# Six quarter-tile places for split weights, and a new order of the seven products of a pair, in a hybrid decoder trunk

## The chip, the cores and the metric

The kernel runs on one core of a Trainium2 chip. The metric is the device time of one execution in microseconds (us): the median over several runs. A time "of the profiled execution" is that of the single run in which the hardware profiler also recorded every instruction; its span runs from the first to the last instruction.

## The reference

The kernel computes two decoder layers on 512 tokens of width 1024. Layer 0 mixes by a gated DeltaNet, layer 1 by sliding-window attention, and each layer also attends to 256 memory tokens. The change touches only the feed-forward block that ends each layer (D_MODEL 1024, D_FF 2816):

```python
def swiglu(h, w_gate_up, w_down):
    gu = h @ w_gate_up
    return (jax.nn.silu(gu[..., :D_FF]) * gu[..., D_FF:]) @ w_down
...
        x = x + swiglu(rms_norm(x, ln_ffn[layer]), w_gate_up[layer], w_down[layer])
```

## The kernel before

Activations lie transposed: channels on the 128 partitions, 512 tokens along the row. Every matrix product is made from a high and a low part of both operands: `split` makes the high part by an ACT copy into the fp32r type (`whi`, line 137) and the low part by a VectorE (DVE) subtraction of it (`wlo`, line 150). `mm3` then issues three matmuls for each block of 128x128 weights: high times high, high times low activation, low weight times high activation. So a product can start when `whi` is there, and its third matmul needs `wlo`.

The 22 column blocks of gate and of up are done in two halves of 11 (`f0`). Each half first makes one block plainly (`project`, 24 matmuls of 512 tokens), then goes by pairs of blocks through `quarters`: a gate pair (its result is scaled by `rstd` and put through silu, tile `fg`) and then an up pair (its result is multiplied by the gate's, tile `fu`, and split into activations `acts` by `put`). The first pair of gates in each layer is made plainly, too, so there are 18 gate pairs and 20 up pairs: 38 pairs of `quarters`. After each half the down projection follows (`pj` tiles, matmuls of 512 tokens).

`quarters` does a pair of blocks over two halves of the 512 tokens with seven instead of eight block products. Each product is 4 x 3 = 12 matmuls of 256 tokens; they are named here by the key of the activation that they use: 11, 21, t1, t2, 22, t3, t4. The raw weights of a pair are `a1` (128x1024, tag `wraw`, its halves for 11 and 21), `s1` and `s3` (two sums, tag `ws`, which a POOL DMA makes by adding a second block while it loads) and `last` (for t4). Two DVE additions turn `a1` in place into the weights of t2 and 22. The split weights lie in tiles `whi` and `wlo` of 128x1024, three buffers of each, and a pair takes four: `w0` (11 and 21), `two` (t1 and t3), `w2` (t2 and 22) and `w3` (t4).

Results pass through three PSUM banks of the tag `g` for each pair (six in all): `pa` for 11, t2, t3 and t4 in turn, `pb` for 21, `pc` for t1 and 22. Where a later product is added onto a bank whose value so far is also wanted (11 and t1 and t2), `held` first copies it out (ACT, tile `fs`). So t2 waits for the copy of 11, t3 for the copy of t2, 22 for the copy of t1, and t4 for the DVE operation that reads the bank after t3.

The order of the work on each engine is fixed when the program is built: a scheduler places the instructions of all engines by its own estimate of when they are ready, within the dependencies. Each engine then runs its list strictly in order, and waits for others by semaphores. Loads are issued by the SP queue, the adding loads by POOL.

Of the kernel before, what the change touches and what calls it, by code (L numbers as in the profile page):

```python
# [9 lines left out]
F32 = mybir.dt.float32  # L10
F32R = mybir.dt.float32r
I32 = mybir.dt.int32
AF = mybir.ActivationFunctionType
# [5 lines left out]
P = 128  # L19
T = 512  # L20
# [65 lines left out]
class Builder:  # L86
# [742 lines left out]
    def ffn(self, fp, xp, layer, h, apool, rope=False):  # L829
# [1 line left out]
        nc, a = self.nc, self.a  # L831
        acc = self.acc
        half = FT // 2
        acts, sums = [], []

        col = lambda f, up: a["wgu"][layer, 2 * f + up]

        def gate(f):
            ps = self.project(col(f, 0), h, "pj")
            if f == 0:  # L840
                self.rstd_from(acc)
                self.use(SILU_SIN)
            g = self.t(fp, [P, T], F32, "fg", 4)
            self.tt(nc.vector, g, ps, self.rstd, ALU.mult)
            self.fn(g, g, AF.Silu)
            return g

        def gates(f):
            g = self.quarters(fp, [col(f + i, 0) for i in range(2)], sums, (self.rstd, self.rstd), "fg", 4)
            for x in g:  # L850
                self.fn(x, x, AF.Silu)
            return g

        def put(u):
            n = len(acts)
            acts.append(self.pair(apool) if n < KD else self.pair(fp, f"ac{n}"))
            self.split(u, *acts[-1])

        def add(x, ps, t=slice(0, T)):
            d = self.t(fp, [P, T], F32, "fu", 3)[:, t]  # L860
# [2 lines left out]

        for f0 in (0, half):
            acts.clear()
            g = gate(f0)
            u = self.t(fp, [P, T], F32, "fu", 3)
            self.tt(nc.vector, u, self.project(col(f0, 1), h, "g"), g, ALU.mult)
            put(u)
            for f in range(f0 + 1, f0 + half, 2):  # L870
                if f == 1:
                    g = []
                    for i in range(2):
                        for _ in range(2 - i):
                            sums.append(self.token_sums(fp, layer, len(sums), h))
                        g.append(gate(f + i))
                    sums.append(self.token_sums(fp, layer, len(sums), h))
                else:
                    g = gates(f)
                for u in self.quarters(fp, [col(f + i, 1) for i in range(2)], sums, g, "fu", 3):  # L880
                    put(u)
            self.acc = None
            tail = KD - 2 if f0 and layer else KD
            down = lambda m, j, n, **kw: self.weight(a["wdn"][layer, m][:, (f0 + j) * P:(f0 + j + n) * P], **kw)
            for m in range(tail):
                ps = self.bank("pj")
                for j, n in ((0, 6), (6, 5)):
                    w = down(m, j, n)
                    for k in range(n):
                        self.mm3(ps, w, k, acts[j + k], j + k == 0, j + k == half - 1)  # L890
                add(self.x[m], ps)
                if f0:
                    self.acc = self.accumulate(xp, self.acc, self.x[m], m)
                if rope and f0 == 0 and m == 0:
                    self.rope_tables(fp)
# [49 lines left out]
        parts["21"], parts["22"] = ([x[:, i * q:(i + 1) * q] for x in h[j + 4]] for i in range(2))  # L945
        return parts

    def quarters(self, fp, src, sums, by, tag, bufs):

        nc = self.nc  # L950
        q = T // 2
# [6 lines left out]
        nc.gpsimd.dma_start(s3, a21, accum_op=ALU.add)  # L958
        last = self.t(fp, [P, T], F32, "wraw", 2)
        nc.sync.dma_start(last, a22)  # L960
        w0 = self.weight(None, raw=a1)
        two = [self.t(self.wpool, [P, D], F32R, t, 3) for t in ("whi", "wlo")]
        w1, w4 = ([x[:, i * T:(i + 1) * T] for x in two] for i in range(2))
        self.split(s1, *w1)

        self.tt(nc.vector, a1[:, :T], s1, a1[:, :T], ALU.add)
        self.tt(nc.vector, a1[:, T:], a1[:, :T], a1[:, T:], ALU.add)
        w2 = self.weight(None, raw=a1)
        self.split(s3, *w4)
        w3 = self.weight(None, raw=last)  # L970
        pa, pb, pc = (self.bank("g")[:, :q] for _ in range(3))

        def product(ps, w, i, b, first):

            for j in range(4):
                self.mm3(ps, w, 4 * i + j, sums[j][b], first and j == 0, j == 3, not first)

        def held(ps):
            o = self.t(fp, [P, q], F32, "fs", 3)
            self.copy(o, ps)  # L980
            return o

        u = [self.t(fp, [P, T], F32, tag, bufs) for _ in range(2)]
        product(pa, w0, 0, "11", True)
        p1 = held(pa)
        product(pb, w0, 1, "21", True)
        self.tt(nc.vector, u[0][:, :q], pb, p1, ALU.add)
        product(pc, w1, 0, "t1", True)
        p5 = held(pc)
        product(pa, w2, 0, "t2", False)  # L990
        u2 = held(pa)
        product(pc, w2, 1, "22", False)
        self.tt(nc.vector, u[0][:, q:], pc, u2, ALU.add)
        self.tt(nc.vector, u[0], u[0], by[0], ALU.mult)
        product(pa, w4, 0, "t3", False)
        self.stt(u[1][:, q:], pa, -1.0, p5, ALU.mult, ALU.subtract)
        self.tt(nc.vector, u[1][:, q:], u[1][:, q:], by[1][:, q:], ALU.mult)
        product(pa, w3, 0, "t4", False)
        self.stt(u[1][:, :q], pa, -1.0, by[1][:, :q], ALU.mult, ALU.mult)
        return u  # L1000

    def rstd_from(self, acc, t=slice(0, T)):
        self.use(LN_EXP)
# [208 lines left out]
```

## Time and profile before

| | |
|---|---|
| median of 3 runs | 1216.53 us (1214.99 to 1218.32) |
| profiled execution | 1217.5 us, span 1215.7 us |
| TensorE matmuls (PE), weight loads (PEld) | 1164.1 us (96%), 1003.6 us (83%) |
| VectorE (DVE), ACT, POOL | 818.1 us (67%), 616.0 us (51%), 83.2 us (7%) |
| mean granted TensorE clock | 0.996 |
| DMA | 151.22 MB, mean 124 GB/s |

Columns of the trace's views: a row of the timeline gives start, duration, engine, source line, operation, tiles (output <- inputs), and in brackets the idle time of the engine before it with what ended it. "PE" is the matmul, "PEld" the load of its stationary operand, which goes ahead of it; matmuls are pipelined, so their durations overlap and the distance between starts is what one costs. The chain of waits is followed back from the last instruction, at each step to what released it. The time for the feed-forward pairs lies in four stretches, which begin at about 339, 511, 859 and 1031 us of the span.

### The profile page before, as it was taken

How to read it: one execution, taken by the hardware profiler on the slowest of the kernel's cores; microseconds unless marked ns; L12 is line 12 of the kernel's file. 1: busy time of each engine (PE TensorE's matmuls, PEld its weight loads, DVE VectorE, ACT ScalarE, POOL GpSimd, SP SyncE). 2: the span in 40 equal slices, each digit the busy share in tenths (PEclk: the TensorE clock that was granted, in tenths of full speed). 3: DMA queues.
4: the chain of work that ended last, by engine and by line, in shares of the span. 5: the costliest groups of instructions: out<-in, count | busy, mean ns of one | idle time of the engine just before them, and what ended most of it. 6: DMA issues, size and time to landing. Idle time of an engine off the chain costs nothing.

```text
span 1215.7 us, 19269 instructions
## 1 busy us (share of the span) xinstructions
PE 1164.1 (96%) x7410; PEld 1003.6 (83%) x7410; DVE 818.1 (67%) x1482; ACT 616.0 (51%) x1174; POOL 83.2 (7%) x93
## 2 busy tenths in 40 slices
PE   7999999999999999999999999999999999999997
PEld 6888777877898988888988876788898888898886
DVE  6753977667877775477765767768678644677644
ACT  7578562565555532255543546766455422555423
POOL 0310000000111101011100000010111100111000
PEclk9999999999999999999999999999999999999999
DMA  7424252324556536456533420153466633666232
GB/s 294 140 88 138 88 126 75 121 78 154 167 139 165 142 102 164 115 142 168 135 84 96 130 87 28 44 139 104 119 152 169 156 96 99 151 154 163 75 98 89
DMA packets 72944, 151.22 MB, mean 124 GB/s; under 512 B 16732, under 2 KB 19444, under 8 KB 72852
## 3 DMA queue, kind: packets, MB, share of 16 engines
q1 hardware_dynamic: 61908, 130.06, 35.1%
q0 software_dynamic: 10944, 19.93, 10.2%
q8 instruction: 58, 0.95, 0.3%
q14 instruction: 34, 0.28, 0.1%
HBM read 143.00 MB, written 6.96 MB: 123 GB/s over the span
## 4 chain that ended last, share of the span: by engine, by line
PE 82%; DVE 10%; ACT 3%; issue 3%; DMA 1%; SPq 0%; DVEq 0%; ACTq 0%
PE pj L143 42%; PE g L143 32%; PE sc L143 6%; DVE wlo L150 5%; PE pt L147 1%; ACT fs L137 1%; PE g L147 1%; DVE fu L150 1%; DVE fg L150 1%; ACT sm L131 1%; DMA wraw<-in_wmk 1%; DVE btmp L150 1%; ACT whi L137 0%; DVE big L150 0%; DMA big<-basein 0%
## 5 line engine op out<-in xcount | busy, mean ns | idle before, releaser
L137 ACT ACTIVATE whi<-wraw 128x1024 fp32r<-128x1024 f32 (+3 forms) x249 | 225.6, 921 | 254.2 <-PE pj L143 173.4
L150 DVE TENSOR_TENSOR wlo<-wraw,whi 128x1024 fp32r<-128x1024 f32 (+3 forms) x249 | 259.6, 1054 | 96.3 <-ACT whi L137 95.4
L143 PE MATMUL pj<-h,whi 128*128 128x512 f32 (+1 forms) x676 | 266.1, 395 | 0.2
L143 PE MATMUL pj<-h,wlo 128*128 128x512 f32 (+1 forms) x676 | 265.1, 392 | 1.1 <-DVE wlo L150 1.1
L143 PE MATMUL pj<-l,whi 128*128 128x512 f32 (+1 forms) x676 | 265.5, 393 | 0.0
L143 PE MATMUL g<-T,whi 128*128 128x256 f32 x1216 | 222.8, 281 | 0.0
L143 PEld LDWEIGHTS g<-T,whi 128*128 128x128 f32 x1216 | 187.3, 189 | 0.4
L143 PE MATMUL g<-T,wlo 128*128 128x256 f32 x608 | 171.7, 282 | 0.7 <-DVE wlo L150 0.7
L143 PE MATMUL g<-h,wlo 128*128 128x256 f32 (+1 forms) x516 | 150.2, 302 | 18.9 <-DVE wlo L150 18.9
L143 PE MATMUL g<-h,whi 128*128 128x256 f32 (+1 forms) x516 | 154.5, 302 | 7.6 <-ACT fs L137 7.6
L143 PEld LDWEIGHTS pj<-h,wlo 128*128 128x128 f32 x676 | 127.4, 188 | 29.4 <-DVE wlo L150 2.9
L143 PE MATMUL g<-l,whi 128*128 128x256 f32 (+1 forms) x516 | 150.4, 294 | 0.0
L143 PEld LDWEIGHTS pj<-h,whi 128*128 128x128 f32 x676 | 127.1, 188 | 28.1 <-issue 2.6
L143 PEld LDWEIGHTS pj<-l,whi 128*128 128x128 f32 x676 | 127.2, 188 | 26.6 <-issue 1.5
L137 ACT ACTIVATE fs<-g 128x256 f32<-128x256 f32 x114 | 43.8, 384 | 152.1 <-PE g L143 151.9
L143 PEld LDWEIGHTS g<-h,wlo 128*128 128x128 f32 x516 | 95.3, 189 | 28.2 <-DVE wlo L150 25.8
L143 PEld LDWEIGHTS g<-T,wlo 128*128 128x128 f32 x608 | 114.5, 188 | 1.1 <-DVE wlo L150 1.1
L143 PEld LDWEIGHTS g<-h,whi 128*128 128x128 f32 x516 | 97.6, 189 | 17.1 <-ACT fs L137 14.2
L143 PEld LDWEIGHTS g<-l,whi 128*128 128x128 f32 x516 | 97.8, 190 | 2.9 <-issue 0.5
L957 POOL DMA_DIRECT2D ws<-in_wgu x38 | 33.2, 873 | 951.8 <-DVE wlo L150 259.5
L150 DVE TENSOR_TENSOR fu<-g,fs 128x256 f32<-128x256 f32 x40 | 17.0, 425 | 64.2 <-PE g L143 64.2
L150 DVE TENSOR_TENSOR fu<-pj,rstd 128x512 f32<-128x512 f32 (+1 forms) x34 | 22.4, 659 | 49.9 <-PE pj L143 49.9
(346 smaller groups left out, 1671.3 us busy)
## 6 DMA issues: line engine op xcount, KB each, us to landing
wraw<-in_wgu SPq DMA_DIRECT2D x50, 512.0 KB, 4.1
ws<-in_wgu SPq DMA_DIRECT2D x76, 256.0 KB, 2.9
ws<-in_wgu POOLq DMA_DIRECT2D x76, 256.0 KB, 6.3
wraw<-in_win SPq DMA_DIRECT2D x26, 512.0 KB, 3.6
wraw<-in_wdn SPq DMA_DIRECT2D x32, 384.0 KB, 3.2
wraw<-in_wdn SPq DMA_DIRECT2D x32, 320.0 KB, 2.9
wraw<-in_wgu SPq DMA_DIRECT2D x38, 256.0 KB, 6.0
wraw<-in_wout SPq DMA_DIRECT2D x16, 512.0 KB, 3.6
```

Source lines behind the costliest of these rows:

```text
L131: ins = self.nc.scalar.activation(out, in_, func, **kw).ins
L137: self.copied = self.nc.scalar.activation(out, in_, AF.Copy, **kw).ins
L143: return self.nc.tensor.matmul(out, lhsT, rhs, start=start, stop=stop, skip_group_check=more).ins
L147: return self.nc.tensor.transpose(out, in_, self.ident[:k, :k]).ins
L150: return eng.tensor_tensor(out=out, in0=a, in1=b, op=op).ins
L957: nc.gpsimd.dma_start(s1, a22, accum_op=ALU.add)
```

## The change

Only `ffn` and `quarters` change. The diff, with lines left out where they are context:

```diff
--- before.py
+++ after.py
@@ -831,7 +831,7 @@
         nc, a = self.nc, self.a
         acc = self.acc
         half = FT // 2
-        acts, sums = [], []
+        acts, sums, open_pairs, places = [], [], [], []
 
         col = lambda f, up: a["wgu"][layer, 2 * f + up]
 
@@ -845,17 +845,37 @@
             self.fn(g, g, AF.Silu)
             return g
 
-        def gates(f):
-            g = self.quarters(fp, [col(f + i, 0) for i in range(2)], sums, (self.rstd, self.rstd), "fg", 4)
-            for x in g:
-                self.fn(x, x, AF.Silu)
-            return g
-
         def put(u):
             n = len(acts)
             acts.append(self.pair(apool) if n < KD else self.pair(fp, f"ac{n}"))
             self.split(u, *acts[-1])
 
+        def ring():
+
+            if not places:
+                for _ in range(3):
+                    two = [self.t(self.wpool, [P, D], F32R, t, 3) for t in ("whi", "wlo")]
+                    places.extend(tuple(x[:, i * T:(i + 1) * T] for x in two) for i in range(2))
+            places.append(places.pop(0))
+            return places[-1]
+
+        def begin(f, up, by, tag, bufs, then):
+
+            o = [self.t(fp, [P, T], F32, tag, bufs) for _ in range(2)]
+            steps = self.quarters(fp, [col(f + i, up) for i in range(2)], sums, by, o, ring)
+            next(steps)
+            end()
+            next(steps)
+            open_pairs.append((steps, then, o))
+            return o
+
+        def end():
+            if open_pairs:
+                steps, then, o = open_pairs.pop()
+                next(steps, None)
+                for x in o:
+                    then(x)
+
         def add(x, ps, t=slice(0, T)):
             d = self.t(fp, [P, T], F32, "fu", 3)[:, t]
             self.tt(nc.vector, d, ps, self.rstd[:, t], ALU.mult)
@@ -863,6 +883,7 @@
 
         for f0 in (0, half):
             acts.clear()
+            places.clear()
             g = gate(f0)
             u = self.t(fp, [P, T], F32, "fu", 3)
             self.tt(nc.vector, u, self.project(col(f0, 1), h, "g"), g, ALU.mult)
@@ -876,9 +897,9 @@
                         g.append(gate(f + i))
                     sums.append(self.token_sums(fp, layer, len(sums), h))
                 else:
-                    g = gates(f)
-                for u in self.quarters(fp, [col(f + i, 1) for i in range(2)], sums, g, "fu", 3):
-                    put(u)
+                    g = begin(f, 0, (self.rstd, self.rstd), "fg", 4, lambda x: self.fn(x, x, AF.Silu))
+                begin(f, 1, g, "fu", 3, put)
+            end()
             self.acc = None
             tail = KD - 2 if f0 and layer else KD
             down = lambda m, j, n, **kw: self.weight(a["wdn"][layer, m][:, (f0 + j) * P:(f0 + j + n) * P], **kw)
@@ -945,7 +966,7 @@
         parts["21"], parts["22"] = ([x[:, i * q:(i + 1) * q] for x in h[j + 4]] for i in range(2))
         return parts
 
-    def quarters(self, fp, src, sums, by, tag, bufs):
+    def quarters(self, fp, src, sums, by, u, ring):
 
         nc = self.nc
         q = T // 2
@@ -958,46 +979,41 @@
         nc.gpsimd.dma_start(s3, a21, accum_op=ALU.add)
         last = self.t(fp, [P, T], F32, "wraw", 2)
         nc.sync.dma_start(last, a22)
-        w0 = self.weight(None, raw=a1)
-        two = [self.t(self.wpool, [P, D], F32R, t, 3) for t in ("whi", "wlo")]
-        w1, w4 = ([x[:, i * T:(i + 1) * T] for x in two] for i in range(2))
-        self.split(s1, *w1)
-
-        self.tt(nc.vector, a1[:, :T], s1, a1[:, :T], ALU.add)
-        self.tt(nc.vector, a1[:, T:], a1[:, :T], a1[:, T:], ALU.add)
-        w2 = self.weight(None, raw=a1)
-        self.split(s3, *w4)
-        w3 = self.weight(None, raw=last)
         pa, pb, pc = (self.bank("g")[:, :q] for _ in range(3))
 
-        def product(ps, w, i, b, first):
-
+        def product(ps, raw, b, first):
+
+            w = ring()
+            self.split(raw, *w)
             for j in range(4):
-                self.mm3(ps, w, 4 * i + j, sums[j][b], first and j == 0, j == 3, not first)
+                self.mm3(ps, w, j, sums[j][b], first and j == 0, j == 3, not first)
 
         def held(ps):
             o = self.t(fp, [P, q], F32, "fs", 3)
             self.copy(o, ps)
             return o
 
-        u = [self.t(fp, [P, T], F32, tag, bufs) for _ in range(2)]
-        product(pa, w0, 0, "11", True)
+        product(pa, a1[:, :T], "11", True)
         p1 = held(pa)
-        product(pb, w0, 1, "21", True)
+        product(pc, s1, "t1", True)
+        p5 = held(pc)
+        yield
+
+        self.tt(nc.vector, a1[:, :T], s1, a1[:, :T], ALU.add)
+        product(pa, a1[:, :T], "t2", False)
+        u2 = held(pa)
+        product(pb, a1[:, T:], "21", True)
         self.tt(nc.vector, u[0][:, :q], pb, p1, ALU.add)
-        product(pc, w1, 0, "t1", True)
-        p5 = held(pc)
-        product(pa, w2, 0, "t2", False)
-        u2 = held(pa)
-        product(pc, w2, 1, "22", False)
+        self.tt(nc.vector, a1[:, T:], a1[:, :T], a1[:, T:], ALU.add)
+        product(pc, a1[:, T:], "22", False)
         self.tt(nc.vector, u[0][:, q:], pc, u2, ALU.add)
         self.tt(nc.vector, u[0], u[0], by[0], ALU.mult)
-        product(pa, w4, 0, "t3", False)
+        product(pa, s3, "t3", False)
         self.stt(u[1][:, q:], pa, -1.0, p5, ALU.mult, ALU.subtract)
         self.tt(nc.vector, u[1][:, q:], u[1][:, q:], by[1][:, q:], ALU.mult)
-        product(pa, w3, 0, "t4", False)
+        yield
+        product(pa, last, "t4", False)
         self.stt(u[1][:, :q], pa, -1.0, by[1][:, :q], ALU.mult, ALU.mult)
-        return u
 
     def rstd_from(self, acc, t=slice(0, T)):
         self.use(LN_EXP)
```

Three things are different. First, the split weights of a half's pairs lie in three `whi` and three `wlo` tiles taken once, as six places of a quarter each (128x512), used in turn: each product splits its own 128x512 of raw weights into the next place just before its matmuls in program order. The splits of 1024 columns become two of 512. A place is written again for the sixth product after it. Second, the products come in the order 11, t1, t2, 21, 22, t3, t4. Third, `quarters` is a generator that stops after t1 and after t3: `begin` issues 11 and t1 of a pair, then `end` finishes the pair before it (its t4 and its last operations), and then t2 to t3 of the new pair follow.

How this moves instructions is seen at two places in the first half of layer 0. The first is the hand-over from one pair to the next on PE. The numbers are those of the buffers, in order of creation: g_4000 is bank `pa` of the pair that ends, g_4133 and g_4134 are `pa` and `pb` of the next. Before:

```order
L143 MATMUL g_4000<-T_3283,wlo_3985 128x256
L143 MATMUL g_4133<-h_2803,whi_4113 128x256
L143 MATMUL g_4133<-l_2804,whi_4113 128x256
L143 MATMUL g_4134<-h_2961,whi_4113 128x256
L143 MATMUL g_4134<-l_2962,whi_4113 128x256
L143 MATMUL g_4133<-h_2803,wlo_4114 128x256
L143 MATMUL g_4133<-h_2841,whi_4113 128x256
L143 MATMUL g_4133<-l_2842,whi_4113 128x256
L143 MATMUL g_4133<-h_2841,wlo_4114 128x256
L143 MATMUL g_4000<-T_3182,whi_3996 128x256
```

The first row ends t3 of the old pair. Four matmuls with `whi` of the new pair (two of 11, two of 21) follow, then the first with `wlo`, and after eight matmuls t4 of the old pair. Now, at the hand-over between the pair with bank g_3681 and the one with g_3816 (`pa`) and g_3818 (`pc`); the rows left out are the rest of each product's twelve:

```order
L143 MATMUL g_3681<-T_3283,wlo_3305 128x256
L143 MATMUL g_3816<-h_2803,whi_3304 128x256
L143 MATMUL g_3816<-l_2804,whi_3304 128x256
L143 MATMUL g_3816<-h_2803,wlo_3305 128x256
...
L143 MATMUL g_3816<-h_2921,wlo_3305 128x256
L143 MATMUL g_3818<-T_3182,whi_3306 128x256
...
L143 MATMUL g_3818<-T_3283,wlo_3307 128x256
L143 MATMUL g_3681<-T_3182,whi_3306 128x256
...
L143 MATMUL g_3681<-T_3283,wlo_3307 128x256
L143 MATMUL g_3816<-T_3182,whi_3302 128x256
```

After t3 of the old pair come the twelve of 11 and the twelve of t1 of the new pair, then t4 of the old pair, then t2 of the new one. 21, 22 and t3 follow, and then the next pair's 11: seven products for each pair, everywhere in the same order.

The second place is VectorE's list around the end of an up pair, the results of which are `fu`; `wlo` rows are splits, `wraw` rows the additions in place, `l` rows the splits of activations. Before:

```order
L150 TENSOR_TENSOR fu_4136<-g_4135,fs_4191 128x256
L150 TENSOR_TENSOR fu_4136<-fu_4136,fg_4003 128x512
L150 TENSOR_TENSOR wlo_4253<-wraw_4242,whi_4252 128x1024
L153 SCALAR_TENSOR_TENSOR fu_4137<-g_4133,fs_4177 128x256
L150 TENSOR_TENSOR l_4235<-fu_4136,h_4234 128x512
L150 TENSOR_TENSOR fu_4137<-fu_4137,fg_4004 128x256
L150 TENSOR_TENSOR wlo_4257<-ws_4244,whi_4256 128x512
```

The split of the next pair's first 1024 columns (wlo_4253) stands behind the addition and the multiplication that follow product 22 of the old pair. Now:

```order
L150 TENSOR_TENSOR wlo_3307<-wraw_4070,whi_3306 128x512
L150 TENSOR_TENSOR wraw_4070<-ws_4072,wraw_4070 128x512
L153 SCALAR_TENSOR_TENSOR fu_3805<-g_3816,fg_3670 128x256
L150 TENSOR_TENSOR wlo_3303<-ws_4072,whi_3302 128x512
L150 TENSOR_TENSOR l_4000<-fu_3805,h_3999 128x512
L150 TENSOR_TENSOR wlo_3303<-wraw_3943,whi_3302 128x512
L150 TENSOR_TENSOR fg_3933<-g_3946,fs_3962 128x256
L150 TENSOR_TENSOR wlo_3305<-wraw_4070,whi_3304 128x512
L150 TENSOR_TENSOR fg_3933<-g_3947,fs_4018 128x256
```

Here the pair in work has the results fg_3933, and wraw_4070 belongs to the pair after it: its splits for 11 (first row), t1 (fourth) and t2 (eighth) stand ahead of, or between, the two additions that follow 21 and 22 of the pair in work.

## The prediction

> **What bounds the kernel now.** I read the page's busy shares first, then the chain of waits, then the waits of the weight loads, and last the timeline at the places that these name.
>
> ```profile
> PE 1164.1 (96%) x7410; PEld 1003.6 (83%) x7410; DVE 818.1 (67%) x1482; ACT 616.0 (51%) x1174; POOL 83.2 (7%) x93
> PEclk9999999999999999999999999999999999999999
> ```
>
> PE looks full, but these durations overlap, so the gaps have to be read from starts. The chain of waits in layer 1's first half, for one pair (start, us, what):
>
> ```profile
> 888.98 0.44 DVE fu L150
> ...
> 889.47 0.57 issue
> 890.04 1.23 DVE wlo L150
> 891.27 0.04 issue
> 891.32 5.52 PE g L143 x44
> ...
> 896.86 0.39 ACT fs L137
> 897.25 0.04 issue
> 897.30 2.89 PE g L143 x22
> ...
> 901.35 1.23 DVE wlo L150
> ```
>
> The chain leaves PE twice in a period of 901.35 - 890.04 = 11.31 us. The first time it goes through VectorE: product 22 ends, VectorE adds (888.98), multiplies (the 0.57 called issue) and only then splits the next pair's 1024 columns for 1.23 us. The second time it goes through ACT's copy `fs` of t2, for which t3 waits. The waits of the weight loads over the whole run (us in total, times, longest):
>
> ```profile
> PEld g L143 <- DVE wlo L150: 26.9, 36, 0.8
> PEld g L143 <- ACT fs L137: 14.2, 32, 0.4
> ```
>
> So the loss repeats 36 and 32 times, about once in each of the 38 pairs. What one costs is seen at the starts of the weight loads:
>
> ```profile
> 890.25 0.19 PEld L143 LDWEIGHTS g<-h,whi 128*128 128x128 f32 x1
> 890.37 0.19 PEld L143 LDWEIGHTS g<-l,whi 128*128 128x128 f32 x1
> 891.32 0.19 PEld L143 LDWEIGHTS g<-h,wlo 128*128 128x128 f32 x1 [0.76 <-DVE wlo L150]
> 891.42 0.19 PEld L143 LDWEIGHTS g<-h,whi 128*128 128x128 f32 x1
> ...
> 896.54 0.31 PEld L143 LDWEIGHTS g<-T,whi 128*128 128x128 f32 x2
> 897.29 0.19 PEld L143 LDWEIGHTS g<-h,whi 128*128 128x128 f32 x1 [0.44 <-ACT fs L137]
> 897.40 0.19 PEld L143 LDWEIGHTS g<-T,wlo 128*128 128x128 f32 x1
> ```
>
> Undisturbed, loads start 0.12 us apart (890.25, 890.37). Across the first stall it is 0.95 us, then 0.10: the loss is 0.83 - 0.02 = 0.81 us. Across the second, the last of the two loads of the row at 896.54 starts at 896.66, the next at 897.29, then 897.40: 0.63 - 0.12 - 0.01 = 0.50 us. A pair without either takes 11.31 - 1.31 = 10.0 us, which is 84 matmuls of 0.119 us; a product of twelve takes 1.43 us. The chain's pieces agree: (5.52 - 2.89) / 22 = 0.1195 us for one.
>
> **The change part by part.** *The order of products.* With 1.43 us for each, a bank's earlier value is now read out while other products run: between 11 and t2 lie t1 and the old pair's t4 (2.9 us), between t1 and 22 three products (4.3 us), between t2 and t3 lie 21 and 22 (2.9 us), and between t3 and t4 the next pair's 11 and t1 (2.9 us). What has to fit in is a copy or a VectorE operation of 256 columns:
>
> ```profile
> L137 ACT ACTIVATE whi<-ws x76: 610/614/636, 333.1 to 1131.5; 128x512 fp32r<-128x512 f32 x76
> L137 ACT ACTIVATE fs<-g x114: 383/384/386, 340.2 to 1139.1; 128x256 f32<-128x256 f32 x114
> ```
>
> 0.38 us for the copy, and up to 0.61 us for a split that stands before it on ACT, make 1.0 of 2.9 us. The second stall goes: 32 x 0.50 = 16.0 us. What covers it is two products of other banks; without that cover it costs the 0.50 again.
>
> *The places.* A place is free when the product six before has ended, so 5 x 1.43 = 7.2 us are left for its two halves, 0.61 us on ACT and about 0.69 us on VectorE. That is ample if VectorE's list, which runs strictly in order, gets there. VectorE's own pace, from the starts of neighbours:
>
> ```profile
> 426.23 1.22 DVE L150 TENSOR_TENSOR wlo<-wraw,whi 128x1024 fp32r<-128x1024 f32 x1
> 427.37 0.42 DVE L153 SCALAR_TENSOR_TENSOR fg<-g,fs 128x256 f32<-128x256 f32 x1
> 427.70 0.69 DVE L150 TENSOR_TENSOR wlo<-ws,whi 128x512 fp32r<-128x512 f32 x1
> 428.30 0.42 DVE L150 TENSOR_TENSOR fg<-fg,rstd 128x256 f32<-128x256 f32 x1
> 428.63 0.69 DVE L150 TENSOR_TENSOR wraw<-ws,wraw 128x512 f32<-128x512 f32 x1
> ```
>
> 1.14 us for 1024 columns, 0.60 for 512, 0.33 for 256. Each pair trades two splits of 1024 for four of 512: 4 x 0.60 - 2 x 1.14 = +0.12 us. An up pair then has 12 operations of 512 (seven splits, two additions, one multiplication, two activation splits) and 5 of 256: 7.2 + 1.7 = 8.9 us of the 10.0; a gate pair 10 and 5: 7.7 us. I walked the new list through an up pair, with 0 at the start of its 11, results ready at the ends of products (1.43, 2.9, 4.3, 5.7, 7.2, 8.6, 10.0) and the paces above. As an estimate from these rows the splits are done so: t3's at 2.5 (needed 8.6), 22's at 3.1 (7.2), the next 11's at 3.7 (10.0), the next t1's at 5.4 (11.4), t4's at 7.0 (12.9), the next t2's at 8.4 (14.3). VectorE's reading of t3, behind which t4 stands, is done by 10.7 (12.9). The least slack is 2.2 us. The first stall goes, too: 36 x 0.81 = 29.2 us (two of the 36 are a little shorter; I let that stand against rounding).
>
> *The hand-over to the down projection.* Today its third matmul waits for a split:
>
> ```profile
> 437.88 0.40 PE L143 MATMUL pj<-l,whi 128*128 128x512 f32 x1
> 438.56 0.51 PE L143 MATMUL pj<-h,wlo 128*128 128x512 f32 x1 [0.28 <-DVE wlo L150]
> 438.90 0.40 PE L143 MATMUL pj<-h,whi 128*128 128x512 f32 x1
> ```
>
> Such matmuls start 0.23 us apart (65.00 us for 286 in the last row of the rival on loads), so 0.68 + 0.34 - 2 x 0.23 = 0.56 us are lost, four times. The first down split now waits only for a product that ends at least two before the end of t3; hi and lo of 768 columns fit into 2.9 us. From 0 to 2.2 us are won; I take 2. Work that the change adds on PE: none, the same 84 matmuls.
>
> *Loads.* Buffers are freed later, since the split for 22 is now the last reader of `a1`, done about 3 us into its own pair. The next load into that buffer is for the pair after next, whose 11 starts at 20.0: it has some 15 us less a split.
>
> ```profile
> wraw<-in_wgu SPq DMA_DIRECT2D x50, 512.0 KB, 4.1
> ws<-in_wgu SPq DMA_DIRECT2D x76, 256.0 KB, 2.9
> ws<-in_wgu POOLq DMA_DIRECT2D x76, 256.0 KB, 6.3
> ```
>
> 4.1 us for `a1`; 2.9 + 6.3 us for a sum, whose buffer is likewise asked for some 18 us ahead. On SP's list the loads stand in the order in which their buffers come free, so none that is early waits behind a late one for more than 3 us. I cost this at nothing.
>
> The sum: 29.2 + 16.0 + 2.0 = 47.2 us. Against the profiled execution's 1217.5 us (a span of 1215.7 and 1.8 around it) that is 1170.3; that execution lies 1.0 above the median of the runs, so 1169.3 from there. I forecast **1170 us**. The idle time of the weight loads alone, 26.9 + 14.2 = 41.1 us, is the low end of the gain: 1175.4 from the median.
>
> A rule that speaks against more and shorter operations stands in the Trainium skill, VectorE: DVE Perf Modes, section The DRAIN you can't avoid: the next operation does not start until the pipeline of the one before is empty, and its rules ask for few operations. In the rows above the next start comes 0.60 us after that of an operation shown as 0.69 us long, so the shown durations do not add up. If they did, the rival that comes next would decide.
>
> **The rivals.** *VectorE becomes the bound.* With full durations an up pair has 12 x 0.69 + 5 x 0.42 = 10.4 us of VectorE against 10.0 of PE, a gate pair 9.0. Were the 0.4 not made up in gate pairs, 20 x 0.4 = 8 us come back: 1178. For it: the margin is small. Against it: the starts, and the gate pairs' 1.0 us to spare.
>
> *One of the two stalls stays in another place.* In VectorE's list an operation that waits for a late product may stand ahead of a split that PE needs, as the addition and the multiplication do now. If the wait for splits stays at its size, 16.0 + 2 are won: 1199. If the wait for a bank stays, 29.2 + 2: 1186. Against it: the slack of 2.2 us and more.
>
> *The change does not do what it says.* If a half of a tile could be written only when its other half is read out, places would be whole tiles again. One product more would have to end, and 4 x 1.43 = 5.7 us would still cover 1.3 us of splitting; so even then little is lost. What would leave 1217 is a spacing of matmuls that grows by 1.3 us a pair when PE is never idle.
>
> *The loads become the bound, slower.* The rows of two pairs and of a down projection (us, busy of each engine, clock, DMA share, GB/s):
>
> ```profile
> 901.35:912.64 11.29, 10.49 (x87) 10.09 (x86) 7.91 (x14) 5.87 (x10) 1.75 (x2) 1.00 0.66 156
> 912.64:923.95 11.31, 10.52 (x87) 10.11 (x86) 9.04 (x17) 5.87 (x10) 1.72 (x2) 1.00 0.66 170
> 440.70:505.70 65.00, 65.00 (x286) 53.25 (x285) 38.68 (x57) 16.19 (x21) 3.55 (x4) 1.00 0.51 139
> ```
>
> A pair needs 0.66 x 11.3 = 7.5 us of all DMA engines; at 10.0 us that is 75%. If packed traffic made this time longer than a pair lasts, it would set the period. It costs time against before from 11.3 us on, half as much again; at 12 us, 36 x 0.7 = 25 us more: 1242. Against it: a quarter of the DMA time is left, and 15 us for each load. That a PE without pauses is clocked lower is not seen: 65 us of unbroken matmuls ran at 1.00.
>
> **How the numbers follow.** Forecast 73% (its own range 1166 to 1176: the low end of the gain, and 3 us of the runs' scatter); VectorE the bound 9%; one stall left 9%; no effect 4%; slower 5%. All of the first three are faster by over 0.3% (3.6 us, about what a measurement of this kernel tells from no change): 0.91. Within 0.3%: 0.04. Slower: 0.05. The range is 1165 to 1186: it leaves out the 1199 case, no effect and slower, under 2 in 10, and takes in 1178 and the left bank wait.
>
> **What would show it.** In the changed kernel's waits of the weight loads, the two rows on `wlo` and `fs` should all but vanish, PE's period for a pair should be 10.0 us, the chain should run through PE alone in the pairs, and VectorE's rows should show waits for PE, not the reverse. VectorE's busy time should grow by about 5 us in all. If PE waits for `wlo` with VectorE busy ahead of it, the VectorE rival is right; if for `wlo` with ACT or a DMA behind it, the loads. If the stalls vanish and the time does not fall, the spacing of matmuls was not what I read.

## The result

The changed kernel takes **1169.89 us** (median of 4 runs, 1169.53 to 1173.29), the kernel before 1216.3 us (4 runs, 1214.99 to 1218.32) on the same chip: a ratio of **0.9623**, 95% interval 0.9601 to 0.9646. The forecast was 1170 us, the range 1165 to 1186.

The page of the profile after, in the rows that answer to those of before (busy time of each engine; the granted TensorE clock in 40 slices; the loads with KB and median us from issue to landing):

```profile
PE 1144.2 (98%) x7410; PEld 997.9 (85%) x7410; DVE 835.7 (72%) x1558; ACT 630.4 (54%) x1250; POOL 82.9 (7%) x93
PEclk9999999999999999999999999999999999999998
wraw<-in_wgu SPq DMA_DIRECT2D x50, 512.0 KB, 4.0
ws<-in_wgu SPq DMA_DIRECT2D x76, 256.0 KB, 3.5
ws<-in_wgu POOLq DMA_DIRECT2D x76, 256.0 KB, 4.7
```

The chain of waits after, layer 1 (start, us, what). Where it left PE twice in every pair, it now runs through PE alone for nine pairs, the down projection, and ten pairs:

```profile
834.03 88.48 PE g L143 x744
923.21 1.51 PE g L143 x12
924.72 65.27 PE pj L143 x285
989.99 103.91 PE g L143 x852
```

88.48 / 744 = 0.119 us for a matmul, the undisturbed spacing. Of the waits of the weight loads (us in total, times, longest) both rows of before, 26.9 us on `wlo` and 14.2 us on `fs`, are gone. The only such wait left in the pairs and hand-overs is:

```profile
PEld g L143 <- DVE fu L153: 1.1, 4, 0.3
```

It is new: t4 at the end of each half, where no next pair stands between t3 and t4. The four waits of 0.7 us of the down projections for a split (`PEld pj` on `wlo`) are gone as well. Two periods of a pair (columns: window, length, busy us of PE, PEld, DVE, ACT, POOL with counts, clock, DMA share, GB/s):

```profile
860.00:870.00 10.00, 10.00 (x86) 10.00 (x85) 9.30 (x18) 6.31 (x13) 2.60 (x3) 1.00 0.78 198
870.00:880.00 10.00, 10.00 (x86) 10.00 (x85) 8.64 (x17) 6.31 (x13) 1.63 (x2) 1.00 0.77 182
```

The span fell from 1215.7 to 1167.7 us, by 48.0. Read in the two chains from the start of a half's pairs to the long row of its down projection (in the third half from 859.05 to 960.99 before, from 834.03 to 924.72 after), 11.3, 12.2, 11.25 and 12.2 us of it lie in the four halves with their hand-overs, 46.9 us in all. Another 2.0 us lie ahead of the first pair, in code that the change does not touch, and -0.9 us in the rest.

### The profile page after: what moved, and what is told of

It is laid out like the page before. It is cut to its first block, busy times and chain, and to the rows that moved or that the text cites. A ratio compares the mean times of both kernels' runs of the same rounds, so it can differ in the third digit from the quotient of the medians.

```text
span 1167.7 us, 19451 instructions
## 1 busy us (share of the span) xinstructions
PE 1144.2 (98%) x7410; PEld 997.9 (85%) x7410; DVE 835.7 (72%) x1558; ACT 630.4 (54%) x1250; POOL 82.9 (7%) x93
## 4 chain that ended last, share of the span: by engine, by line
PE 89%; DVE 5%; ACT 3%; DMA 1%; issue 0%; SPq 0%; DVEq 0%; ACTq 0%
PE pj L143 43%; PE g L143 39%; PE sc L143 6%; DVE wlo L150 1%; PE pt L147 1%; PE g L147 1%; ACT sm L131 1%; DMA wraw<-in_wmk 1%; DVE btmp L150 1%; ACT whi L137 1%; DVE big L150 0%; ACT T L137 0%; DVE sm L739 0%; PE qk L143 0%; DMA big<-basein 0%
## 5 line engine op out<-in xcount | busy, mean ns | idle before, releaser
L137 ACT ACTIVATE whi<-wraw 128x512 fp32r<-128x512 f32 (+3 forms) x325 | 243.4, 755 | 286.7 <-PE pj L143 190.2
L150 DVE TENSOR_TENSOR wlo<-wraw,whi 128x512 fp32r<-128x512 f32 (+3 forms) x325 | 272.8, 848 | 108.0 <-ACT whi L137 102.4
L143 PEld LDWEIGHTS g<-h,wlo 128*128 128x128 f32 x516 | 98.0, 190 | 2.5 <-issue 0.2
L137 ACT ACTIVATE whi<-ws 128x512 fp32r<-128x512 f32 x76 | 48.1, 633 | 49.5 <-PE g L143 41.2
L150 DVE TENSOR_TENSOR wlo<-ws,whi 128x512 fp32r<-128x512 f32 x76 | 52.2, 686 | 7.4 <-ACT whi L137 7.3
```

Of the source, the lines that this page charges most:

```text
L137: self.copied = self.nc.scalar.activation(out, in_, AF.Copy, **kw).ins
L143: return self.nc.tensor.matmul(out, lhsT, rhs, start=start, stop=stop, skip_group_check=more).ins
L150: return eng.tensor_tensor(out=out, in0=a, in1=b, op=op).ins
```

## The experiments

All ratios are to the kernel before on the same chip, with a 95% interval. "Planner" in the expectations is the scheduler that fixes the order of each engine's list when the program is built.

| kernel | us | ratio |
|---|---|---|
| the change | 1169.9 | 0.9623 (0.9601 to 0.9646) |
| whole tiles, pairs overlap | 1171.1 | 0.9617 (0.9594 to 0.9640) |
| three places | 1172.7 | 0.9629 (0.9603 to 0.9656) |
| six places, old order, no overlap | 1174.1 | 0.9660 (0.9646 to 0.9674) |
| six places, new order, no overlap | 1180.7 | 0.9695 (0.9678 to 0.9711) |
| before, 1024-column splits in halves | 1187.1 | 0.9768 (0.9751 to 0.9784) |
| two places | 1232.5 | 1.0132 (1.0115 to 1.0148) |
| before, one multiplication held back | 1241.5 | 1.0212 (1.0197 to 1.0227) |
| before, product 22 last | 1272.9 | 1.0475 (1.0458 to 1.0491) |

### Places alone, overlap alone

**Places alone.** The products of a pair in the old order, a pair finished before the next begins:

```diff
-  11, t1, [t4 of the pair before], t2, 21, 22, t3    each from ring()
+  11, 21, t1, t2, 22, t3, t4                         each from ring()
```

It was first run in a form in which a pair was finished only after the next one's products; that form multiplies the up pair by gates that have not been through silu, so it changes the computation by that.

> Six places as in the change, but the products of a pair stay in the order 11, 21, t1, t2, 22, t3, t4 and a pair is finished before the next is begun. Theory (two separate stalls; the places remove the one on the low halves of the splits, the order the one on the bank of t3): the wait on wlo (26.9 us before) falls under 5 us, the wait on fs stays near 14 us; 1170 + 16 = 1186 us (1180 to 1195). Rival A (the order alone makes the gain, the places are only its form): both waits stay, 1210 to 1220 us. Rival B (the places alone make the gain): 1168 to 1175 us.

It took 1173.8 us, ratio 0.9642 (0.9624 to 0.9660). The form with silu in its place:

> Six places, the order of products of the kernel before (11, 21, t1, t2, 22, t3, t4), each pair finished before the next is begun, and Silu ahead of the gating as in the reference. Theory after the first four runs (both stalls of a pair come from too little room for whole splits; quarter places or overlap each take them away): 1172 to 1178 us, with 0.1 to 0.2 us a pair left at t4's bank. Rival (my reading before: the bank wait is another matter, cured by the order alone): 1186 us with the wait on fs near 14 us.

1174.1 us, inside the range of the theory. In both the wait on `fs` is gone as well as that on `wlo`, so the places alone remove both stalls, and the first expectation's two separate stalls are refuted. Nine pairs of it in the chain:

```profile
836.97 89.65 PE g L143 x744
```

That is 0.1205 instead of 0.1189 us for a matmul, 0.13 us for the 84 of a pair: t4's first weight load comes 0.27 us behind its neighbour instead of 0.12, with only eight matmuls of the next 11 between it and t3.

**Overlap alone.** Whole tiles of 1024 columns in three buffers, as before, but the next pair's 11 and 21 ahead of the old pair's t4:

```diff
-  11, 21, t1, t2, 22, t3, t4
+  11, 21, [t4 of the pair before], t1, t2, 22, t3
```

> Whole tiles of 1024 columns in three buffers as before the change, but pairs overlap: 11, 21, t4 of the pair before, t1, t2, 22, t3. So t3 still stands one product behind t2, as before; what changes is that the next pair's first split can stand ahead of the add and the multiply behind product 22. Theory: the wait on wlo falls under 8 us, that on fs stays near 14 us; 1186 us (1180 to 1196). Rival (the quarter places are needed for the first stall): the wait on wlo stays over 20 us, 1205 to 1225 us.

1171.1 us: not to be told from the change. Both expectations were wrong; the wait on `fs` went too, although t3 still stands one product behind t2. Nine pairs:

```profile
835.40 87.07 PE g L143 x732
```

0.1189 us again (these are nearly nine pairs). So the quarter places and the overlap are two cures of one illness, and the change takes both.

**The change without the overlap**, so that t4 follows t3 in the program:

```diff
             next(steps)
-            end()
             next(steps)
             open_pairs.append((steps, then, o))
+            end()
```

> The change with the overlap alone undone: t4 stands right behind t3 of its own pair in the program, the rest (places, order 11, t1, t2, 21, 22, t3) as in the change. t4 then waits for VectorE to read t3's bank. Theory: where nothing stands between t3 and t4 each pair loses about what the fs wait cost, 0.5 us: 38 x 0.5 = 19, 1189 us; the planner has put eight matmuls of the next 11 (0.95 us) between t3 and t4 in this kernel, which covers that, so 1170 to 1178 us. Rival (the overlap is the core of the change): 1189 us or more, with a wait on VectorE's fu or fg of over 15 us in the weight loads.

1180.7 us, above the expectation of 1170 to 1178. The covered wait (t4) is small, 0.08 us a pair. Another came up: without the old pair's t4 between them, only t1 lies between 11 and t2, and t2 waits for the copy of 11. The first weight load of t2 from the timeline, which starts 0.38 us behind its neighbour:

```profile
873.35 0.30 PEld L143 LDWEIGHTS g<-T,whi 128*128 128x128 f32 x2 [0.19 <-ACT fs L137]
```

And nine pairs from the chain of waits:

```profile
337.63 91.15 PE g L143 x744
```

91.15 / 744 = 0.1225 us, 0.30 us a pair more than in the change, 11 us in 38 pairs: the whole difference. The new order needs the overlap. Both together are 4 us ahead of the old order without overlap, with intervals that touch; quarter places in the old order with overlap were not run.

### What the two stalls of before were

The results send one back to the trace of before. From its timeline, ACT ahead of the first stall (start, us, engine and operation, and in brackets the idle time before it with what ended it), and VectorE and PE at the second:

```profile
888.78 1.06 ACT L137 ACTIVATE whi<-wraw 128x1024 fp32r<-128x1024 f32 x1 [0.80 <-PE g L143]
...
896.11 1.83 DVE L150 TENSOR_TENSOR wlo<-wraw,whi 128x1024 fp32r<-128x1024 f32 x2 [0.24 <-ACT whi L137]
...
896.66 0.40 PE L143 MATMUL g<-T,whi 128*128 128x256 f32 x2
897.30 0.39 PE L143 MATMUL g<-h,whi 128*128 128x256 f32 x1 [0.24 <-ACT fs L137]
897.52 0.28 PE L143 MATMUL g<-T,wlo 128*128 128x256 f32 x1
```

First stall: the high half of the next pair's split starts only when a product of PE has ended. That product is 22: its last matmul with a high half ends at 888.75, while t3 still runs, so the split is written into the tile that 22 read last. The high half is ready at 889.84, so the low half could not have started more than 0.2 us before its 890.04, whatever stood in VectorE's list. Second stall: `h` operands belong to 11, 21 and 22, `T` operands to t1 to t4. The waiting matmul is therefore the first of **22**, and the copy is that of **t1** out of bank `pc`; it stands in PE's list between the second and third matmul of t2. t2's own low half (1024 columns from 896.11, so about 897.3) comes no earlier. In the last pair of the second half of each layer no matmul of 22 stands there, and the same 0.50 us are a wait for that low half:

```profile
617.39 0.39 PE L143 MATMUL g<-T,wlo 128*128 128x256 f32 x1 [0.34 <-DVE wlo L150]
```

The prediction had read this wait as t3 behind the copy of t2.

So both stalls are one chain: a high half of 1.06 us, then a low half of 1.22 us, begun too late for the products that need them. Three runs take this apart.

**The chain made shorter**, nothing else: in the kernel before,

```diff
-        w0 = self.weight(None, raw=a1)
+        w0 = self.weight(None, raw=a1, parts=2)
...
-        w2 = self.weight(None, raw=a1)
+        w2 = self.weight(None, raw=a1, parts=2)
```

> The kernel before, whole tiles, old order, no overlap, one thing changed: the two splits of 1024 columns (for 11 and 21, for t2 and 22) are made as two splits of 512 each within the same tile. A product then waits only for its own half. Theory (what PE waits for in both stalls is the length of a 1024-column split behind a tile that came free late): the low half of product 11 is ready 0.54 us earlier, so 0.81 us become 0.27 us (VectorE's add and multiply still stand ahead of it): 36 x 0.54 = 19 us; the low half that t2 waits for comes earlier too, and the planner no longer puts a matmul of 22 behind two of t2, so the 16 us of the fs wait go: 1216 - 35 = 1181 us (1174 to 1188). Rival (the tile that comes free late is what costs, so only more places or overlap help): over 1205 us. Rival (splitting alone does all): 1168 to 1172 us.

1187.1 us, inside 1174 to 1188: 28 of the 46 us with two arguments. The waits of the weight loads in products:

```profile
PEld g L143 <- DVE wlo L150: 13.6, 50, 1.0
```

Of the 50 waits 34 are of 11 (8.3 us) and 16 of t2's low half (5.2 us). ACT and VectorE at the first stall, from the timeline:

```profile
891.81 1.16 ACT L137 ACTIVATE whi<-wraw 128x512 fp32r<-128x512 f32 x2 [0.93 <-PE g L143]
...
892.46 0.69 DVE L150 TENSOR_TENSOR fu<-fu,fg 128x512 f32<-128x512 f32 x1
893.07 0.69 DVE L150 TENSOR_TENSOR wlo<-wraw,whi 128x512 fp32r<-128x512 f32 x1
```

The row on `fs` is gone, since the scheduler no longer moves a matmul of 22 into t2. The first stall is 0.29 us (0.81 before), and here the prediction's reason holds: the high half is ready by 892.4, the low half waits for the multiplication until 893.07. Most of the 6 us by which the run lies above 1181 are the low half of t2 that PE still awaits in those 16 pairs: 0.40 us are lost behind the row at 878.08 in that trace, and 16 x 0.40 = 6.4 us.

**VectorE's list alone**: in the kernel before, the multiplication behind 22 is made to wait until the next pair's low half has been split. The silu or the splits of the pair's two results (`then`) are held back with it. The next pair calls `late` behind its first split:

```diff
-        self.tt(nc.vector, u[0], u[0], by[0], ALU.mult)
...
+        def late(after):
+            ins = self.tt(nc.vector, u[0], u[0], by[0], ALU.mult)
+            if after is not None:
+                self.nosync(ins, after)
+            for x in u:
+                then(x)
```

> The kernel before, with one thing moved: the multiplication behind product 22 (0.60 us of VectorE) is held back until the first low half of the next pair has been split. The planner also moves two matmuls of t1. If VectorE's list is the cause of the first stall (the prediction's reading), the wait on wlo shrinks by 0.6 us in each of 36 pairs: 22 us, 1194 us (1187 to 1200). If room is the cause (the high half can only start when product 22 gives its tile free, and is ready at 889.84 in the trace of before, 0.2 us ahead of the low half's start at 890.04), at most 0.2 x 36 = 7 us are won: 1209 to 1217 us.

1241.5 us, slower than before and outside both expectations. Waits of the weight loads:

```profile
PEld g L143 <- ACT whi L137: 38.4, 50, 1.7
PEld g L143 <- DVE wlo L150: 13.2, 18, 0.9
PEld g L143 <- ACT fs L137: 7.1, 16, 0.4
```

The first split of a pair on ACT and VectorE, from the timeline:

```profile
890.31 1.06 ACT L137 ACTIVATE whi<-wraw 128x1024 fp32r<-128x1024 f32 x1 [1.54 <-PE g L143]
...
891.40 1.23 DVE L150 TENSOR_TENSOR wlo<-wraw,whi 128x1024 fp32r<-128x1024 f32 x1 [0.39 <-ACT whi L137]
```

On the disputed point the run is clear: with nothing ahead of it, VectorE stands idle for 0.39 us until the high half is there. The high half, so the late tile, held the first stall, as the second theory said: from the last matmul of 22 to the first of 11 with a low half it is 2.65 us here (875.93 to 878.58) and 2.73 before (888.59 to 891.32). What that theory left out is t2: in 16 pairs its high half is now awaited for 1.7 us, 27 of the 38.4 us, and its low half for another 0.7 us (most of the 13.2). The other 34 waits on `whi`, of 0.34 us, are of two matmuls of t1 that the scheduler put between those of 11. ACT makes t2's high half behind the copy of t1, and in an up pair VectorE ends the two additions that feed it 6.4 us after the start of the pair's first low half (877.22 to 883.6); in the kernel before it was 4.5 us (890.04 to 894.59). That the held-back multiplication alone moved them is not shown, since the silu and the splits moved with it and the scheduler moved other work too.

**The late tile**: in the kernel before, 22 behind t4, with the addition and the multiplication that follow it.

```diff
-  11, 21, t1, t2, 22, t3, t4
+  11, 21, t1, t2, t3, t4, 22
```

> Whole tiles of 1024 columns in three buffers and no overlap of pairs, as before; product 22 alone moved behind t4. The next pair's first split then takes the tile that t3 gives free, with t4 and 22 (2.9 us) to cover 1.06 us on ACT and 1.14 us on VectorE, instead of t3 alone. Theory (room): the wait on wlo falls under 6 us; the planner still puts two matmuls of 22 two matmuls behind t1, so the wait on fs stays near 14 us; 1186 us (1180 to 1196). Rival (VectorE's list): the wait on wlo stays over 20 us, 1205 to 1225 us.

1272.9 us, far outside. But the first stall is gone, as the theory had it. The product 11 waits in loads `g<-h,wlo`; their row in the page of before (count | busy us, mean ns | idle us before them, and what ended most of it):

```profile
L143 PEld LDWEIGHTS g<-h,wlo 128*128 128x128 f32 x516 | 95.3, 189 | 28.2 <-DVE wlo L150 25.8
```

and in that of this run:

```profile
L143 PEld LDWEIGHTS g<-h,wlo 128*128 128x128 f32 x516 | 100.9, 196 | 2.5 <-issue 0.2
```

The 25.8 us were 34 of the 36 waits on `wlo` before; none is left. This does not tell the tile from VectorE's list, since the addition and the multiplication now stand behind the low half as well (at 894.84 and 895.78, the low half at 893.22); the run before this one does. The time is lost at t2 instead, which now waits for its high half, for its low half (all 34 waits on `wlo` in the second row) and for copies:

```profile
PEld g L143 <- ACT whi L137: 42.9, 34, 1.9
PEld g L143 <- DVE wlo L150: 14.7, 34, 0.7
PEld g L143 <- ACT fs L137: 14.5, 45, 0.5
```

VectorE and ACT ahead of t2, from the timeline:

```profile
892.28 0.42 DVE L153 SCALAR_TENSOR_TENSOR fu<-g,fs 128x256 f32<-128x256 f32 x1 [3.80 <-PE g L143]
...
898.79 0.69 DVE L150 TENSOR_TENSOR wraw<-wraw 128x512 f32<-128x512 f32 x1
...
899.51 1.58 ACT L137 ACTIVATE whi<-wraw 128x1024 fp32r<-128x1024 f32 x2
```

VectorE idles 3.80 us at a reading of t3, then works almost without a pause, and the second of the additions that feed t2's split comes late in this work, at 898.79; the high half starts at 899.51. So a tile that comes free earlier is not enough when the list behind it has stood waiting for a product. That is the prediction's idea of the in-order list, at another place than it was put; it is read from this trace, and no run tests it alone.

### How many places

The ring cut to its first n places, 3 or 2:

```diff
                     places.extend(tuple(x[:, i * T:(i + 1) * T] for x in two) for i in range(2))
+                del places[n:]
```

> The change with three places instead of six, all else the same. A place is then free when the product three before has ended, so 2 x 1.43 = 2.9 us are left for 0.61 us on ACT and 0.69 us on VectorE. Theory (the two halves and what stands ahead of them in the lists fit where the slack read from the walk allows 2.2 us of delay, and here about 1.5 us are left): some products wait, 1172 to 1195 us. Rival A (slack is ample): 1168 to 1172 us. Rival B (every product waits, since ACT and VectorE are busy 6.3 and 9.5 of 10.0 us and their lists run in order): over 1216 us.

> The change with two places instead of six. A place is then given free when the product two before has ended, so one product, 1.43 us, is there for 0.61 us on ACT and 0.69 us on VectorE, 1.30 us with hardly anything for what stands ahead of them in the lists. Theory (room decides): nearly every product of the 7 x 38 = 266 waits, for 0.3 to 0.8 us: 1170 + 80 to 210 = 1250 to 1380 us, slower than before. Rival (the gain of the change is in the order, room matters little): under 1200 us.

Three places: 1172.7 us, not to be told from six. That is 0.7 us above the range of rival A and inside that of the theory, but in the pairs of its trace a single product waits for a split (0.7 us), so the slack is ample, as rival A has it. Two: 1232.5 us, below the expected 1250 but slower than before, with these waits:

```profile
PEld g L143 <- ACT whi L137: 36.1, 77, 1.7
PEld g L143 <- DVE wlo L150: 15.7, 40, 0.4
```

117 waits in 266 products, 52 us. A half split needs 0.61 + 0.69 = 1.3 us. Two products of cover (2.9 us) are plenty, one (1.43 us) fails nearly every second time. Three quarter places are half the room of the three whole tiles of before: it is not the amount of room that was short.

### How near VectorE is to the bound

Multiplications of 512 columns into a tile that nobody reads, two or four in each pair of the change, and two in the kernel of whole tiles with overlap:

```diff
+        more = lambda: self.tt(nc.vector, xx, self.rstd, self.rstd, ALU.mult)
```

> The change with two more VectorE multiplications of 512 columns in each pair (into a tile that nobody reads). By the paces from the starts (0.60 us for 512 columns, 0.33 for 256) an up pair asks 10.1 us and a gate pair 8.9 us of VectorE, 9.5 on the mean, against 10.0 us of PE; the slack of 2.2 us carries the 0.1 over: 1169 to 1174 us. Rival (the shown durations add up, 0.69 and 0.42 us): 11.8 and 10.4, 11.1 us on the mean: 1170 + 38 x 1.1 = 1212 us.

> The change with four more VectorE multiplications of 512 columns in each pair. By the starts 11.3 us in an up pair, 10.1 in a gate pair, 10.7 on the mean, so VectorE sets the period: 1170 + 38 x 0.7 = 1197 us (1190 to 1210). Rival (the shown durations add up): 13.2 and 11.8, 12.5 on the mean: 1265 us. Rival (VectorE has more room than either): under 1180 us.

> The kernel with whole tiles and overlapping pairs (11, 21, t4 of the pair before, t1, t2, 22, t3), with two more VectorE multiplications of 512 columns in each pair. VectorE's work in a pair is 0.12 us less than with quarter places, but a split of 1024 columns has to be ready as a whole. Theory (places of a quarter buy slack, not time): the waits on wlo or whi come back, 1176 to 1200 us, more than the change with the same two multiplications. Rival (quarter places buy nothing): 1169 to 1174 us, like the other.

1173.6 us (0.9644, 0.9628 to 0.9659), 1177.1 us (0.9673, 0.9658 to 0.9688) and 1173.2 us (0.9646, 0.9626 to 0.9667). Windows of the first:

```profile
880.00:890.00 10.00, 10.00 (x87) 10.00 (x86) 9.97 (x20) 6.46 (x13) 1.73 (x2) 1.00 0.78 184
890.00:900.00 10.00, 10.00 (x87) 10.00 (x86) 10.00 (x20) 6.30 (x13) 1.73 (x2) 1.00 0.78 183
```

VectorE is busy to the last tenth, with 20 operations in 10 us, and PE loses nothing there. The shown durations of the 20 of the first row, 15 of 0.68 and 5 of 0.42 us, add up to 12.3 us. Nine pairs of layer 0 take 88.48 us for 744 matmuls in the chain, as they do in the change.

But the run is not what was planned. The multiplications depend on nothing, and the scheduler put all 76 beside the first half of each layer (about 3 in every 10 us of its pairs, the rest just ahead of or behind them) and none beside the second halves. So the first halves bear more than the expectation asked, the second nothing, and the totals do not test its sums. The first pair of layer 1 starts at 838.19 instead of 834.03, behind some of these multiplications. In the second run about half of the 152 stand beside the pairs of the first halves, and as many behind them, 37 of these in one row:

```profile
L150 DVE TENSOR_TENSOR raw<-rstd 128x512 f32<-128x512 f32 x37 | 25.5, 690 | 0.9
```

(window 940 to 1000 of that trace). The third run has its multiplications beside the first halves, too; there whole tiles stand the load as well as quarter places do, so the places buy no slack that this load would show.

## Why the prediction was right, and where it was not

**The sum.** 47.2 us were forecast for pairs and hand-overs, 46.9 were found there. The size of each stall was measured at the starts of the weight loads, and both went entirely, so the sum holds whatever had caused them. That both went although the cause of each was misread (below) was luck. Two of the 36 waits on `wlo`, called a little shorter, are the second stall (617.39 is one); with 34 of each the stalls are 44.5 instead of 45.2 us. The forecast of 1170 against 1169.9 is in part luck: the 2.0 us ahead of the first pair are no effect of the change, and make up for the missing 0.3 and the 0.9 lost elsewhere.

**The period** of 10.0 us, PE alone on the chain, loads without effect (a DMA share of 0.77 to 0.78, 0.75 had been worked out) and the clock at 1.00 came as forecast. The loads were tested by no run of their own.

**The first stall** was put down to the wrong step: "only then splits the next pair's 1024 columns", VectorE's list. The high half on ACT behind the tile of 22 held it; the list was worth at most 0.2 of 0.81 us, and holding the multiplication back won 0.08. The list became the limit only when the split was halved.

**The second stall** was misread: not t3 behind the copy of t2, but the first matmul of 22 behind the copy of t1, in the middle of t2. The step "between t2 and t3 lie 21 and 22 (2.9 us)" was thus no cure for it, and the gain of 16.0 us was not the order's: places alone give it too. The rival "one of the two stalls stays" (1186 or 1199) rested on two independent causes and had less for it than the 9% said.

**Bank waits.** The covers between 11 and t2 and between t3 and t4 are real: without the overlap 0.30 us a pair come back, where I had named 0.50 for a lost cover.

**The places.** "5 x 1.43 = 7.2 us are left" is true and not needed: 2.9 us do. The rival that halves of a tile cannot be written apart was answered as it was worked out, little would be lost; whole tiles with the overlap lose nothing.

**VectorE.** "Should grow by about 5 us" was mis-sized: it grew by 17.6 us (818.1 to 835.7), ACT by 14.4. I had counted starts (+0.12 us a pair). The profile counts shown durations: 152 splits of 0.69 instead of 76 of 1.22 are +12 us; the other 6 I can't account for. The expected sign, VectorE waiting for PE, is not there either. VectorE's waits after, in the first half of layer 1 (836 to 922 us):

```profile
DVE wlo L150 <- ACT whi L137: 5.4, 13, 0.7
DVE fu L150 <- PE g L143: 2.6, 2, 2.4
```

In the kernel before, the pairs of that half had these (868.6 to 957 us):

```profile
DVE fu L150 <- PE g L143: 12.7, 8, 2.3
DVE fg L150 <- PE g L143: 8.0, 4, 2.0
```

Before, the list stood 20.7 us behind products; now it hardly does, and VectorE is busy for 9.3 and 8.6 of 10.0 us. The rival that it becomes the bound is refuted by the run with 20 operations in 10 us. Its rule stands in the Trainium skill, VectorE: DVE Perf Modes, section The DRAIN you can't avoid; by it those 20 would need 12.3 us, an estimate that takes the shown durations to add up. The same section says that a next operation which is not held starts earlier, and the starts 0.60 us apart agree with that.

## What to carry to other kernels

A wait in the profile names what came last, not what began late: follow the chain back to the first instruction that started on a release, and see by its operands which product it is, before pricing a cure. A row of waits can mix products, so it has to be split by operands before one says that a stall stayed or went. What counts for a split of weights is its length against the products between the release of its place and its use; overlapping the pairs, or quarter places, each bought almost all of the gain, and one of them would have been enough; halving the pieces of the split within the old tiles bought 28 of 46 us. A reordering that looks local moves the whole plan where a scheduler fills lists: of the three that kept the whole tiles (the overlap, the held-back multiplication, 22 last) two made the kernel slower, by 26 and 57 us.

## What was not expected of the hardware

A pause of TensorE can cost more than its length. In the kernel with the held-back multiplication PE paused twice:

```profile
885.24 0.50 PE L143 MATMUL g<-T,whi 128*128 128x256 f32 x2 [1.48 <-ACT whi L137]
...
886.50 0.39 PE L143 MATMUL g<-T,wlo 128*128 128x256 f32 x1 [0.52 <-DVE wlo L150]
```

The windows behind it (columns as above):

```profile
885.00:887.00 2.00, 1.23 (x8) 1.03 (x9) 1.78 (x2) 0.71 (x2) 1.74 (x2) 1.00 0.26 22
887.00:888.00 1.00, 1.00 (x8) 1.00 (x8) 0.05 (x1) 0.00 (x0) 0.00 (x0) 0.67 1.03 184
888.00:889.00 1.00, 1.00 (x6) 1.00 (x6) 0.00 (x0) 0.38 (x1) 0.00 (x0) 0.50 0.86 86
889.00:890.00 1.00, 1.00 (x6) 1.00 (x6) 0.00 (x0) 0.00 (x0) 0.00 (x0) 0.50 0.87 205
890.00:891.00 1.00, 1.00 (x8) 1.00 (x7) 0.41 (x1) 0.69 (x1) 0.00 (x0) 0.63 1.06 291
```

The granted clock is 0.50 for some 3.4 us, and weight loads start 0.21 instead of 0.12 us apart. It does not follow every such pause. In the waits of the weight loads these two are 1.68 and 0.73 us; 1.69 and 0.72 us at 910.69 and 911.95 of the same trace left it at 1.00:

```profile
912.00:914.00 2.00, 2.00 (x17) 2.00 (x18) 0.49 (x1) 0.39 (x1) 0.48 (x1) 1.00 0.88 158
```

What makes the difference is not shown. In the kernel with 22 last the mean clock of the span of 1270 us is 0.983, against 0.996 before; as an estimate that is 1270 x 0.013 = 17 of the 57 us that it lost. The Trainium skill, TensorE: Matmul & The Clock Gate, section What's actually happening, has a clock that is halved after an idle window of about 3.4 us and comes back after a busy one. The 3.4 us at half clock agree; but here PE was idle for about 2 us in all, in two pieces, not for a whole window.
